# A first stage that also builds other layers' conditioning: 21 background chunks moved forward, and the ring of tiles split in two

## The chip, the cores and the metric

The kernel runs on one core of one Trainium2 chip. The metric is the device time of one execution in microseconds (us), the median of several runs. Lower is better. TensorE is called PE here, VectorE DVE, ScalarE ACT, GpSimd POOL and SyncE SP, as in the profile.

## The reference: what is computed

A backbone block with two layers works on 256 noisy latent tokens and 256 context tokens of width 2048. Every layer's modulation comes from a conditioning vector:

```python
def ada_mods(cvec, w, b):
    m = jax.nn.silu(cvec) @ w + b
    return jnp.split(m, N_MOD, axis=-1)
```

The first two parts (shift and scale of layer 0's mixer) are needed before anything else: the normalised input is `h * (1 + scale) + shift`, and the first layer's projections multiply that by large weight matrices. The other parts of the same kind (gate, and the shift, scale and gate of the two feed-forward blocks and of layer 1) are needed only later in the program, one after another. Layer 0 then runs eight HGRN2 heads (query, forget gates, values, a chunked scan) beside token-mixing heads, an output projection and a feed-forward block; layer 1 a pooling mixer and a feed-forward block.

## The kernel before

All large products are made in three passes of a reduced float format: a weight tile `raw` arrives from HBM by DMA, ACT casts it to a high part `hi`, DVE subtracts to get the low part `lo` (`load_w`, lines 169 to 187), and PE multiplies high by high, high by low and low by high (`mm`, line 221). A raw tile's buffer can be filled again when its `hi` and `lo` are made. All these DMAs are issued by SP, whose queue takes them strictly in order: one that must wait for its buffer holds back all behind it.

**The first stage** (`startup`, lines 438 to 609) goes through the 16 k-tiles of the input in nine slices: two slices of one k-tile, then seven of two. It overlaps two things. For slice i it computes with PE the first projections (`values`, two groups v0 and v1 with PSUM tiles `mmi`; `forgets`, three groups f0, f1, f2 with tiles `mmf`). Meanwhile it prepares slice i+1: `cond` multiplies the conditioning vector by the weights of shift and scale (tiles `sraw`, 512 KB each, PSUM tile `ps_as`), `transposed` turns the input, and `modulate` brings both together into the k-tiles `xt` that the next v0 reads. A slice of two k-tiles needs eight `sraw`: four in group A (run 0 of `cond`), four in group B (run 1). Within a group PE takes the tile that was loaded last first. The order on PE is written out by hand: v0, A, v1, B with the transposes, f0, the small products of `modulate`, f1, f2; for i = 1 alone it is v0, A, B, v1, so A and B stand back to back. `in_order` ties each step to the one before. All other engines are filled by a scheduler by priority; `high_priority(offset=-LATER)` marks work that is to come last.

The `sraw` tiles and the background's tiles share one ring of seven buffers, tag `a4`; two more buffers, tag `s4`, serve `sraw` in the first stage alone. So `sraw` go round nine buffers.

**The background** (`ada_task`, lines 296 to 339) makes the parts of the modulation that are needed later: 20 tasks of 16 chunks each, 320 in all. A chunk is one DMA of 512 KB (`araw`, line 307) and one DVE instruction that adds `araw` times a scalar to an accumulator `acc` (line 311). After the 16th chunk `last` splits `acc` into two tiles `apart` and sends them through PE. Chunks are taken from a list by `pump`, which `load_w` calls: each load adds `rate` to a credit, and each whole credit takes a chunk, at low priority. `plan(left, loads)` sets the rate so that after so many loads only `left` chunks remain. The heads (`mixer_even`) begin with

```python
        self.plan(LEFT_H, LOADS_H)
```

with LEFT_H = 240 and LOADS_H = 22: 80 chunks over 22 loads. After them `plan(LEFT_M, 38)` takes 50 more over 38 loads. In the first stage the rate is zero: no chunk is taken there.

Of the kernel before, what the change touches and what calls it, by code (L numbers as in the profile page):

```python
# [12 lines left out]
F32 = mybir.dt.float32  # L13
F32R = mybir.dt.float32r
# [5 lines left out]
P = 128  # L20
# [10 lines left out]
LATER = 50  # L31
# [2 lines left out]
STEPS = "f0 f1 f2 q0 s0 i s1 q1 f3 s2 f4 s3 q2 f5 s4 f6 s5 q3 f7 s6"  # L34
LOADS_H = 8 + 4 + 2 * (NH - N_START)
BATCH = 2
NA4 = 7
NS4 = 2
NG4 = 7
NT2 = 9  # L40
N_PRE = 3
FIRST_S = 100
HELD = 1
N_WARM = 1
N_WARM_S = 15
LEFT_H = 240
LEFT_M = 190
# [103 lines left out]
class Builder:  # L151
# [141 lines left out]
    def ada_task(self, task, dst, row):  # L293

        nc = self.nc
        st = {}

        def first():
            st["acc"] = self.ap.tile([P, 1024], F32, tag="a4", bufs=NA4, name="acc")
            nc.gpsimd.memset(st["acc"], 0.0)  # L300
            nc.sync.dma_start(st["acc"][0:1, :], self.I["bada"][task:task + 1, :])

        def chunk(c):
            if c == 0:
                first()
            raw = self.ap.tile([P, 1024], F32, tag="a4", bufs=NA4, name="araw")
            nc.sync.dma_start(raw, self.I["wada"][task * 16 + c])
            acc = st["acc"]

            with self.tc.issue_after(self.norm) if self.norm is not None else nullcontext():  # L310
                nc.vector.scalar_tensor_tensor(acc, raw, self.csil[:, c, 0:1], acc, ALU.mult, ALU.add)  # L311
            if c == KT - 1:
                last()

        def last():
            hi, lo = (self.ap.tile([P, 1024], F32R, tag="a4", bufs=NA4, name="apart") for _ in range(2))
            nc.scalar.copy(hi, st["acc"])
            nc.vector.tensor_sub(lo, st["acc"], hi.bitcast(F32))
            if row:
                g = self.gate_tile()  # L320
                dst.append(g)
                for j in range(2):
                    ps = self.pa.tile([P, 512], F32, tag="ax", name="ps_ada")
                    for i, z in enumerate((hi, lo)):
                        self.mm(ps, self.ones, z[:, 512 * j:512 * j + 512], i == 0, i == 1)
                    nc.scalar.copy(g[:, 512 * j:512 * j + 512], ps)
            else:
                ps = self.pa.tile([P, 512], F32, tag="ax", name="ps_ada")
                rows = self.cp.tile([4, T], F32, tag="crow", bufs=1, name="crow")
                for j in range(4):  # L330
                    for i, z in enumerate((hi, lo)):
                        self.mm(ps[0:4, 0:T], self.hot[:, j], z[:, T * j:T * j + T], j + i == 0, j + i == 4)
                nc.scalar.copy(rows, ps[0:4, 0:T])
                for h in range(2):
                    nc.tensor.transpose(ps[:, T + 4 * h:T + 4 * h + 4], rows[:, h * P:h * P + P], self.ident[0:4, 0:4])
                nc.scalar.copy(dst.rearrange("p (j h) -> p h j", h=2), ps[:, T:T + 8].rearrange("p (h j) -> p h j", h=2))

        for c in range(KT):
            self.bg.append((task // 2, lambda c=c: chunk(c)))
# [100 lines left out]
    def startup(self):  # L440
# [8 lines left out]
        for b in range(4):  # L449
            src = (I["x"] if b < 2 else I["ctx"])[(b % 2) * P:(b % 2) * P + P, :]  # L450
            if b < 2:
                t = self.xp.tile([P, D], F32, tag="x8", name="xraw")
# [43 lines left out]
        def cond(i, run):  # L496
# [8 lines left out]
            for c in range(run * nk, run * nk + nk):  # L505
                src = I["wada_h"][2 * k0 + c] if nk == 1 else I["wada_s"][2 * k0 - 4 + c]
                for h in range(2):
                    self.n_sraw += 1
                    if self.n_sraw % (NA4 + NS4) < NS4:
                        t = self.sp.tile([P, 1024], F32, tag="s4", bufs=NS4, name="sraw")  # L510
                    else:
                        t = self.ap.tile([P, 1024], F32, tag="a4", bufs=NA4, name="sraw")
                    nc.sync.dma_start(t, src[:, 1024 * h:1024 * h + 1024])
                    todo += [(n * c + j, t, j * w % 1024) for j in range(n) if j * w // 1024 == h]
            first = None
# [94 lines left out]
        def in_order(*steps):  # L610
            for fn in steps:
                with self.tc.issue_after(st["last"]) if "last" in st else nullcontext():
                    fn()
                st["last"] = self.first_mm
# [3 lines left out]
        for i, (k0, nk) in enumerate(slices):  # L618
# [10 lines left out]
            steps += [lambda: forgets(i, 0, wf)] + more * [lambda: modulate_first(i + 1)]  # L629
            steps += [lambda h=h: forgets(i, h, wf) for h in range(1, N_START)]  # L630
            in_order(*steps)
            if i in (1, 4):
                with self.tc.issue_after(st["act"]), self.tc.issue_after(st["dve"]):
                    scale_rows(1) if i == 1 else self.lower_bounds()
# [459 lines left out]
    def build(self):  # L1094
        nc, tc = self.nc, self.tc
        pool = tc.tile_pool
        with pool(name="cp", bufs=1) as self.cp, pool(name="wp", bufs=1) as self.wp, \
# [7 lines left out]
            c = {n: col(n) for n in ("sh2_0", "sc2_0", "sh1_1", "sc1_1", "sh2_1", "sc2_1")}  # L1105
            self.NG4, self.NT2 = NG4, NT2
            with pool(name="tp0", bufs=1) as self.tp, pool(name="vp", bufs=1) as self.vp:
# [8 lines left out]
                self.ada(8, c["sc2_1"])  # L1116
                gate2 = self.ada(9, None)
                with pool(name="sp", bufs=1) as self.sp:
                    fbacc = self.startup()
                with pool(name="gp", bufs=1) as self.gp:  # L1120
                    self.mixer_even(fbacc)
                    stat = self.out_proj()
# [31 lines left out]
```

## Time and profile before

| | before |
|---|---|
| median of 3 runs | 2271.59 us (2270.16 to 2273.35) |
| the profiled execution | 2277.5 us |
| its span in the trace | 2275.4 us |
| PE busy, share of the span | 2244.2 us, 99% |
| DVE busy | 1686.8 us, 74% |
| ACT busy | 1101.7 us, 48% |
| HBM read | 578.55 MB, 255 GB/s over the span |

The profiled execution took 5.9 us more than the median of the runs; 2.1 us of its time lie outside its span. In the trace the first stage runs from the start to about 174 us, the heads from there to about 478 us, the token mixing to about 545, the output projection to 685, the first feed-forward block to 1409, the pooling mixer to 1552, the last feed-forward block to the end. A busy PE is not a PE at its peak, but a stretch in which PE is busy throughout can't be shortened by anything that another engine does sooner.

### The profile page before, as it was taken

What the parts mean: (1) busy time and instruction counts of PE and PEld (TensorE: products, weight loads), DVE (VectorE), ACT (ScalarE), POOL (GpSimd) and SP (SyncE); (2) the same over time, 40 slices, a digit from 0 to 9 for tenths busy, and PEclk for the clock granted to TensorE, in tenths of its full rate; (3) what the DMA queues carried; (4) which work ended last, traced back from release to release, by engine and by line L of the source; (5) the groups of instructions that cost most, each with busy time, mean ns of one, the idle gap of its engine ahead of it and who ended that gap; (6) DMA issues with size and microseconds to landing.
All of it is one profiled execution on the core that took longest, in us unless ns stands there. A gap on an engine that the chain in (4) does not pass through costs nothing.

```text
span 2275.4 us, 31649 instructions
## 1 busy us (share of the span) xinstructions
PE 2244.2 (99%) x12532; PEld 1866.1 (82%) x12532; DVE 1686.8 (74%) x2055; ACT 1101.7 (48%) x1484; POOL 37.0 (2%) x47
## 2 busy tenths in 40 slices
PE   9999999999999999999999999999999999999998
PEld 5677788778888878888887888888888888888887
DVE  4669999988868877887888875769964655556655
ACT  4326466554446545544544554445444443443443
POOL 0000000001000000000000000000000000000000
PEclk9999999999999999999999999999999999999999
DMA  9786766777877888888888885646865555555553
GB/s 376 279 300 224 273 254 245 263 278 289 323 278 264 317 307 304 302 319 304 314 317 308 296 307 197 222 171 250 313 228 194 185 187 196 182 192 187 185 190 125
DMA packets 110636, 582.71 MB, mean 256 GB/s; under 512 B 12292, under 2 KB 12420, under 8 KB 66584
## 3 DMA queue, kind: packets, MB, share of 16 engines
q1 hardware_dynamic: 110488, 580.70, 70.4%
q8 instruction: 98, 1.61, 0.3%
q14 instruction: 50, 0.41, 0.0%
HBM read 578.55 MB, written 2.10 MB: 255 GB/s over the span
## 4 chain that ended last, share of the span: by engine, by line
PE 82%; DVE 8%; DMA 5%; issue 2%; ACT 2%; POOL 0%; SPq 0%; DVEq 0%; POOLq 0%; ACTq 0%
PE mma L221 36%; PE mmb L221 34%; PE mmf L221 3%; PE mmn L221 2%; DMA araw<-in_wada 2%; DVE lo L185 2%; DVE acc L311 2%; PE mmi L221 2%; PE ps_as L221 1%; ACT hi L184 1%; DVE kk L758 1%; DVE qg L758 1%; DMA sraw<-in_wada_h 1%; PE ps_ada L221 0%; PE ps_o L221 0%
## 5 line engine op out<-in xcount | busy, mean ns | idle before, releaser
L184 ACT CAST hi<-raw 128x1024 fp32r<-128x1024 f32 (+1 forms) x701 | 733.0, 1047 | 942.1 <-PE mma L221 461.0
L185 DVE TENSOR_TENSOR lo<-raw,hi 128x1024 fp32r<-128x1024 f32 (+1 forms) x701 | 849.8, 1215 | 408.5 <-ACT hi L184 407.0
L221 PE MATMUL mma<-hi,xt 128*128 128x512 f32 x2800 | 873.3, 391 | 0.9 <-DVE q L280 0.9
L221 PE MATMUL mmb<-xt,hi 128*128 128x512 f32 x2304 | 812.8, 397 | 1.1 <-DVE xt L389 0.8
L221 PE MATMUL mmb<-xt,lo 128*128 128x256 f32 x2304 | 648.0, 281 | 0.8 <-DVE lo L185 0.8
L221 PEld LDWEIGHTS mma<-hi,xt 128*128 128x128 f32 x2800 | 525.0, 188 | 111.8 <-DVE q L280 1.3
L221 PE MATMUL mma<-lo,xt 128*128 128x512 f32 x1400 | 547.1, 391 | 2.1 <-DVE lo L185 2.1
L221 PEld LDWEIGHTS mmb<-xt,hi 128*128 128x128 f32 x2304 | 432.8, 188 | 103.8 <-DVE xt L389 1.0
L311 DVE SCALAR_TENSOR_TENSOR acc<-araw,csil,acc 128x1024 f32<-128x1024 f32 x320 | 409.9, 1281 | 62.1 <-DMA araw<-in_wada 59.7
L221 PEld LDWEIGHTS mmb<-xt,lo 128*128 128x128 f32 x2304 | 436.3, 189 | 3.1 <-DVE lo L185 1.1
L221 PEld LDWEIGHTS mma<-lo,xt 128*128 128x128 f32 x1400 | 263.2, 188 | 58.5 <-DVE lo L185 3.2
L221 PE MATMUL mmf<-xt,hi 128*128 128x512 f32 x512 | 165.3, 395 | 0.1
L221 PEld LDWEIGHTS mmf<-xt,hi 128*128 128x128 f32 x512 | 96.0, 188 | 21.0 <-PE mmf L221 0.5
L221 PE MATMUL mmf<-xt,lo 128*128 128x512 f32 x256 | 100.1, 391 | 0.0
L221 PE MATMUL mmn<-hi,xt 128*128 128x256 f32 x416 | 76.0, 283 | 0.0
L221 PEld LDWEIGHTS mmn<-hi,xt 128*128 128x128 f32 x416 | 65.3, 192 | 0.4
L221 PE MATMUL mmn<-lo,xt 128*128 128x256 f32 x208 | 58.9, 283 | 0.0
L221 PEld LDWEIGHTS mmf<-xt,lo 128*128 128x128 f32 x256 | 48.2, 188 | 9.5
L740 ACT COPY both<-kk 128x256 f32<-128x256 f32 x64 | 26.3, 411 | 54.2 <-DVE kk L758 43.3
L389 DVE TENSOR_TENSOR xt<-hup,xt 128x512 fp32r<-128x512 f32 x64 | 43.9, 687 | 7.9 <-ACT xt L388 7.9
L603 DVE TENSOR_TENSOR fbacc<-mmf,fbacc 128x1024 f32<-128x1024 f32 x24 | 29.3, 1221 | 21.9 <-PE mmf L221 21.8
L221 PE MATMUL mmi<-hi,xt 128*128 128x512 f32 x128 | 44.2, 404 | 1.2 <-DVE xt L568 0.6
(187 smaller groups left out, 1347.1 us busy)
## 6 DMA issues: line engine op xcount, KB each, us to landing
araw<-in_wada SPq DMA_DIRECT2D x320, 512.0 KB
raw<-in_w_up SPq DMA_DIRECT2D x128, 1024.0 KB
raw<-in_w_down SPq DMA_DIRECT2D x128, 1024.0 KB
sraw<-in_wada_s SPq DMA_DIRECT2D x56, 512.0 KB
raw<-in_w_out SPq DMA_DIRECT2D x16, 1024.0 KB
raw<-in_w_pool SPq DMA_DIRECT2D x16, 1024.0 KB
raw<-in_w_fb SPq DMA_DIRECT2D x10, 1024.0 KB
raw<-in_w_q SPq DMA_DIRECT2D x8, 1024.0 KB
```

The lines of the kernel that those rows point to most:

```text
L184: nc.scalar.copy(hi, raw[:, o:o + w])
L185: nc.vector.tensor_sub(lo, raw[:, o:o + w], hi.bitcast(F32))
L221: self.first_mm = self.nc.tensor.matmul(out, lhsT, rhs, start=start, stop=stop, **kw).ins
L311: nc.vector.scalar_tensor_tensor(acc, raw, self.csil[:, c, 0:1], acc, ALU.mult, ALU.add)
L389: return self.nc.vector.tensor_sub(x[:, :, lo], src, x[:, :, hi].bitcast(F32))
L603: nc.vector.tensor_add(fbacc[h], ps, fbacc[h])
L740: nc.scalar.copy(o.rearrange("p (s j i) -> p j s i", j=2, i=hh), bass.AP(src.tensor, src.offset, [list(src.ap[0]), [st + hh, 2], [seg, ns] ...
L758: nc.vector.tensor_mul(x, x, m.broadcast_to([P, ns, hh]))
```

## The change

The ring `a4` goes from seven buffers to three. A new ring `b4` has four, so both together take as much memory as before. The ring `s4` of the first stage goes from two buffers to three. In the first stage the `sraw` tiles use `b4` and `s4`, seven buffers together, and background chunks use `a4`, where one buffer is held by the accumulator. After the first stage a chunk with an odd number uses `a4`, one with an even number `b4`; the two `apart` tiles use `b4`.

At the end of the iterations i = 2 to 8 of the first stage three chunks each are taken from the list at low priority, 21 in all. The plan of the heads still leaves 240, so its 22 loads now take 59 chunks and not 80.

```diff
-NA4 = 7
-NS4 = 2
+NA4 = 3
+NB4 = 4
+NS4 = 3
...
+N_EARLY = 3
...
         def chunk(c):
             if c == 0:
                 first()
-            raw = self.ap.tile([P, 1024], F32, tag="a4", bufs=NA4, name="araw")
+
+            ring = ("a4", NA4) if self.first_stage or c % 2 else ("b4", NB4)
+            raw = self.ap.tile([P, 1024], F32, tag=ring[0], bufs=ring[1], name="araw")
             nc.sync.dma_start(raw, self.I["wada"][task * 16 + c])
...
         def last():
-            hi, lo = (self.ap.tile([P, 1024], F32R, tag="a4", bufs=NA4, name="apart") for _ in range(2))
+            hi, lo = (self.ap.tile([P, 1024], F32R, tag="b4", bufs=NB4, name="apart") for _ in range(2))
...
                     self.n_sraw += 1
-                    if self.n_sraw % (NA4 + NS4) < NS4:
+                    if self.n_sraw % (NB4 + NS4) < NS4:
                         t = self.sp.tile([P, 1024], F32, tag="s4", bufs=NS4, name="sraw")
                     else:
-                        t = self.ap.tile([P, 1024], F32, tag="a4", bufs=NA4, name="sraw")
+                        t = self.ap.tile([P, 1024], F32, tag="b4", bufs=NB4, name="sraw")
...
             in_order(*steps)
+            if i >= 2:
+                with self.tc.high_priority(offset=-LATER):
+                    for _ in range(N_EARLY):
+                        self.bg.popleft()[1]()
...
+                    self.first_stage = True
                     fbacc = self.startup()
+                    self.first_stage = False
```

Three places show how the instructions move. Names carry the program's numbers; line numbers after the change are larger by 2 to 8.

SP's queue before, at the loads of one slice of the first stage (the slice whose `ps_as` ran at 112.01 us in the trace of before). The waits in brackets are on semaphores: PE_49 is set by PE, DVE_49 by DVE, Activation_49 by ACT, DMAHW by earlier transfers of the same number:

```order
L174 DMA raw_949<-in_w_is 128x1024 [waits DMAHW1_49,DVE_49]
L174 DMA raw_955<-in_w_fbs 128x1536 [waits DMAHW2_49,DVE_49]
L513 DMA sraw_980<-in_wada_s 128x1024 [waits DMAHW3_49,PE_49]
L513 DMA sraw_982<-in_wada_s 128x1024 [waits DMAHW4_49,PE_49]
L513 DMA sraw_984<-in_wada_s 128x1024 [waits DMAHW5_49,PE_49]
L513 DMA sraw_986<-in_wada_s 128x1024 [waits DMAHW6_49,PE_49]
L513 DMA sraw_1010<-in_wada_s 128x1024 [waits DMAHW7_49]
L513 DMA sraw_1012<-in_wada_s 128x1024 [waits DMAHW0_49,PE_49]
L513 DMA sraw_1014<-in_wada_s 128x1024 [waits DMAHW1_49]
L513 DMA sraw_1016<-in_wada_s 128x1024 [waits DMAHW2_49]
L174 DMA raw_1099<-in_w_is 128x1024 [waits DMAHW3_49,DVE_49]
```

The eight tiles of the slice, sraw_980 to sraw_986 for group A and sraw_1010 to sraw_1016 for group B, stand together, and each one's wait on PE is for tiles of the slice before.

SP's queue after, at the same slice, from the third tile of group A on (group A is sraw_1010 to sraw_1016 here, group B sraw_1040 to sraw_1046):

```order
L517 DMA sraw_1014<-in_wada_s 128x1024
L517 DMA sraw_1016<-in_wada_s 128x1024 [waits DMAHW5_49,PE_49]
L517 DMA sraw_1040<-in_wada_s 128x1024 [waits DMAHW7_49,DMAHW6_49]
L517 DMA sraw_1042<-in_wada_s 128x1024
L517 DMA sraw_1044<-in_wada_s 128x1024 [waits DMAHW0_49]
L311 DMA araw_960<-in_wada 128x1024 [waits DMAHW1_49,DVE_49]
L311 DMA araw_963<-in_wada 128x1024 [waits DMAHW2_49,DVE_49]
L517 DMA sraw_1046<-in_wada_s 128x1024 [waits DMAHW3_49,PE_49]
L311 DMA araw_966<-in_wada 128x1024 [waits DMAHW4_49,DMAHW1_49,DVE_49]
L176 DMA raw_1138<-in_w_is 128x1024 [waits DMAHW5_49,Activation_49]
L176 DMA raw_1144<-in_w_fbs 128x1536 [waits DMAHW6_49,Activation_49]
```

The eighth tile of the slice, sraw_1046, now stands behind two chunks and takes the buffer of sraw_1010, so its wait on PE is for the fourth pair of matmuls of group A of its own slice. The third chunk and the weights of the next slice stand behind it.

ACT before, at the last but one step of `modulate` (xt6 is k-tiles 12 and 13; the inputs of the casts L184 are the weights w_fbs and w_is of the next slices):

```order
L540 COPY sp_1200<-ps_as_1129 128x512
L557 ACTIVATE mtmp_1211<-ps_t_1176,mcol_1207 128x256 x2
L567 CAST xt6_98<-mtmp_1211 128x512
L567 CAST xt6_98<-mtmp_1212 128x512
L184 CAST hi_1257<-raw_1255 128x1024
L184 CAST hi_1261<-raw_1255 128x512
```

ACT after, at the same place:

```order
L544 COPY sp_1239<-ps_as_1168 128x512
L186 CAST hi_1299<-raw_1297 128x1024
L561 ACTIVATE mtmp_1250<-ps_t_1215,mcol_1246 128x256
L186 CAST hi_1305<-raw_1303 128x1024
L561 ACTIVATE mtmp_1250<-ps_t_1215,mcol_1246 128x256
L186 CAST hi_1309<-raw_1303 128x512
L571 CAST xt6_98<-mtmp_1250 128x512
L571 CAST xt6_98<-mtmp_1251 128x512
```

The two casts that make xt6 have moved behind both casts of the weights raw_1303; the buffers that those write are read by PE until the last matmul of f2.

DVE after, at the same step:

```order
L563 TENSOR_SCALAR mtmp_1251<-ps_t_1216,mcol_1246 128x256
L187 TENSOR_TENSOR lo_1306<-raw_1303,hi_1305 128x1024
L187 TENSOR_TENSOR lo_1310<-raw_1303,hi_1309 128x512
L563 TENSOR_SCALAR mtmp_1251<-ps_t_1216,mcol_1246 128x256
L572 TENSOR_TENSOR xt6_98<-mtmp_1250,xt6_98 128x2x256
L607 TENSOR_TENSOR fbacc_214<-mmf_1274,fbacc_214 128x1024
L572 TENSOR_TENSOR xt6_98<-mtmp_1251,xt6_98 128x2x256
```

The low parts of raw_1303 stand ahead of the two instructions that finish xt6, and the addition of f2's result between those two. The same order returns at the step after it (xt7).

## Rows read from the trace of the kernel before

**Rows 1.** Windows: length, busy us per engine, PE clock (1.00 is full), DMA share, GB/s.

```profile
20.00:48.00 28.00, 27.20 (x181) 17.34 (x179) 12.66 (x25) 13.14 (x20) 0.00 (x0) 1.00 1.03 403
48.00:168.00 120.00, 119.61 (x655) 82.98 (x655) 76.82 (x105) 38.12 (x56) 0.95 (x1) 1.00 0.81 297
168.00:478.00 310.00, 301.41 (x2385) 244.51 (x2385) 292.90 (x553) 181.73 (x352) 7.89 (x7) 1.00 0.70 252
sum 2275.40, PE 2244.21 PEld 1866.08 DVE 1686.76 ACT 1101.65 POOL 36.98; mean PE 249.36 PEld 207.34 DVE 187.42 ACT 122.41 POOL 4.11
```

**Rows 2.** Waits of PE over the span: us in total, times, longest us.

```profile
PE ps_sc L221 <- ACT both L740: 5.9, 9, 1.5
PE ps_mx L221 <- DVE vg L843: 3.0, 2, 2.1
```

**Rows 3.** Timeline of one slice: start us, us, engine, line, operation.

```profile
92.42 1.92 PE L221 MATMUL ps_as<-sraw,cst 128*32 128x512 f32 x16
...
97.26 1.92 PE L221 MATMUL ps_as<-sraw,cst 128*32 128x512 f32 x16
...
107.82 1.28 DVE L568 TENSOR_TENSOR xt<-mtmp,xt 128x512 fp32r<-128x512 f32 x2
...
109.20 0.39 PE L221 MATMUL mmi<-hi,xt 128*128 128x512 f32 x1
...
112.01 1.50 PE L221 MATMUL ps_as<-sraw,cst 128*32 128x512 f32 x12
```

**Rows 4.** Timeline where groups A and B stand back to back.

```profile
37.82 1.92 PE L221 MATMUL ps_as<-sraw,cst 128*32 128x512 f32 x16
...
39.91 1.50 PE L221 MATMUL ps_as<-sraw,cst 128*32 128x512 f32 x12 [0.17 <-DMA sraw<-in_wada_s]
```

**Rows 5.** Timeline with SP's issues (SPq), and the PE group before the first.

```profile
53.28 1.92 PE L221 MATMUL ps_as<-sraw,cst 128*32 128x512 f32 x16
...
54.38 5.68 SPq L513 DMA_DIRECT2D sraw<-in_wada_s  x6
...
91.39 0.33 SPq L174 DMA_DIRECT2D raw<-in_w_fbs  x1
...
99.24 1.29 SPq L513 DMA_DIRECT2D sraw<-in_wada_s  x3
```

**Rows 6.** Chain of waits: start us, us from issue to landing.

```profile
0.74 4.86 DMA xraw<-in_x
...
835.09 5.75 DMA araw<-in_wada
...
1413.53 5.85 DMA raw<-in_w_pool
```

**Rows 7.** Windows behind the issue at 91.39, columns as in Rows 1.

```profile
91.90:92.90 1.00, 1.00 (x11) 0.35 (x13) 0.97 (x2) 0.00 (x0) 0.00 (x0) 1.00 0.49 123
92.90:93.90 1.00, 1.00 (x16) 0.23 (x8) 0.85 (x1) 0.00 (x0) 0.00 (x0) 1.00 0.89 326
```

**Rows 8.** Windows from the longest wait of PE on.

```profile
527.80:530.20 2.40, 0.31 (x2) 0.18 (x2) 0.87 (x4) 1.04 (x1) 1.78 (x1) 1.00 0.59 150
530.20:533.60 3.40, 3.40 (x14) 3.19 (x15) 2.70 (x8) 0.00 (x0) 0.00 (x0) 0.50 1.01 419
```

**Rows 9.** Timeline at the last step of `modulate`.

```profile
167.77 0.62 ACT L567 CAST xt<-mtmp 128x512 fp32r<-128x512 f32 x1
167.91 1.83 DVE L185 TENSOR_TENSOR lo<-raw,hi 128x1024 fp32r<-128x1024 f32 x2
...
168.29 0.62 ACT L184 CAST hi<-raw 128x512 fp32r<-128x512 f32 x1
...
169.65 0.69 DVE L568 TENSOR_TENSOR xt<-mtmp,xt 128x512 fp32r<-128x512 f32 x1
...
170.25 1.22 DVE L603 TENSOR_TENSOR fbacc<-mmf,fbacc 128x1024 f32<-128x1024 f32 x1
```

**Rows 10.** Groups of instructions: count, busy us, mean ns, idle before.

```profile
L311 DVE SCALAR_TENSOR_TENSOR acc<-araw,csil,acc 128x1024 f32<-128x1024 f32 x320 | 409.9, 1281 | 62.1 <-DMA araw<-in_wada 59.7 <-DMA acc<-in_bada 0.2
```

## The prediction, made before the result was known

> **What bounds the kernel now.** I read the windows by stage first. PE is busy for 2244.21 of 2275.40 us, so only 31 us can be won by waits that go away [rows 1]. In the steady part of the first stage PE is busy for 119.61 of 120 us, while DVE is busy for 76.82 and the DMA engines for 0.81 of the time; in the heads PE is busy for 301.41 of 310, DVE for 292.90 [rows 1]. The reader is to see two different stages: in the first, spare time lies on DVE (43 us in 120) and no wait of PE is left; in the heads DVE is nearly full, and PE waits 8.6 us. The waits of PE come next: the longest sum is that of the score products for ACT's copies, 5.9 us in nine waits, and the longest single one 2.1 us, in the token mixing [rows 2]. Last comes the timeline of one slice, since the change sets new waits there: A starts at 92.42, B at 97.26, v0 of the next slice at 109.20, and the next A at 112.01 [rows 3]. So a slice takes 19.6 us of dense PE work, B starts 4.84 us after A, and whatever comes late to A, B or v0 adds to the total one to one.
>
> **What is taken from the heads.** 21 chunks leave the plan of the heads, 1.28 us of DVE each [rows 10], 27 us at most. This is no gain by itself: DVE has to become late for PE to wait, and PE's waits in the heads are 8.6 us in all [rows 1], so 8.6 is the upper end. The order of the instructions tells less: between the same two weight splits of the heads (the 24th and the 78th `lo` of the program) DVE carries 87 chunks before and 82 after, because low-priority chunks run ahead of their plan when their buffers allow. Five chunks are 6.4 us of DVE. If DVE's saving came back to PE by the share in which PE waits there (8.6 of 310), it would be 0.2 us; if all of it came back, 6.4. The score products wait for ACT's copies, which wait for DVE's, in nine places only. I take a gain of 1 us, with -8.6 and +3 as ends (the latter half of the waits of the score products again, if these products, which stand closer together in the new order, find their copies later).
>
> **What the chunks cost in the first stage.** 21 chunks are 27 us of DVE and 21 x 512 KB of DMA, three per slice. DVE has 43 us free in 120. A slice moves eight `sraw` of 512 KB, 512 KB of w_is and 768 KB of w_fbs: 10.5 units of 512 KB, and 13.5 with three chunks. At the 403 GB/s of the window from 20 to 48 us [rows 1], where the queue is full, a unit takes 1.30 us, so a slice takes 13.7 us before and 17.6 after, of its 19.6. It fits, with 2 us to spare. PE does nothing for them. As work the chunks cost nothing; the cover is DVE's idle time and those 2 us.
>
> **Term 1, the shorter ring.** Before, nine buffers serve the eight tiles of a slice, and every tile waits for tiles of the slice before. After, seven serve eight: the eighth tile takes a buffer of group A of its own slice. It is the tile that PE takes first in B. So its load can start only when PE has used that buffer in A, and has to land before B, which starts 4.84 us after A begins. Which of the four it waits for is read from the semaphores of the program: in the seven slices of two k-tiles the fourth used, first, second, third, fourth, second, third. The delay from the start of A to the issue is in two rows: 1.10 us for the first used (53.28 to 54.38) and 1.98 us for the fourth (97.26 to 99.24) [rows 3, 5]; 1.4 and 1.7 lie between.
>
> How long 512 KB take from the issue on an empty queue no row shows alone. Three come near: 1 MB took 4.86 and 5.85, and 512 KB in a stretch of other traffic 5.75 [rows 6]. Without the 1.30 us of the second half the first two give 3.6 and 4.55; I take 4.1, their middle. The low end is from the bytes: after the issue at 91.39 on an idle queue 123 KB had moved by 92.90 and 449 by 93.90, so 524 can't be there before 94.1, 2.7 us after [rows 5, 7]. The high end is 5.75.
>
> A page of the Trainium skill has another price. "DMA: Bandwidth & Descriptors", section "Anatomy of one DMA — SWDGE (gpsimd) path", gives about 2.0 us plus the bytes over 436 GB/s, so 3.2 us for 512 KB as an estimate (for DMAs issued by GpSimd; these are SP's). By it this term would be 0.5 for the six steady slices and 3.1 for the first, 3.6 us and not 8.9.
>
> With 4.1, B is late by (issue + 4.1 - 4.84): 0.36, 0.66, 0.96 and 1.26 us for first to fourth. The six steady slices give 0.36 + 0.66 + 0.96 + 1.26 + 0.66 + 0.96 = 4.9 us (0 at 2.7; 14.8 at 5.75). The first of the seven is worse, since there A and B stand back to back, at 37.82 and 39.91 [rows 4]. Its eighth tile is issued at 37.82 + 1.98 = 39.80 and lands at 43.9: B is 4.0 us late (2.6 at 2.7; 5.65 at 5.75). What is late next behind the waiting DMA in SP's queue is the next slice's w_fbs and `sraw`; they are needed 13 us later and more, so nothing follows from it.
>
> **Term 2, the clock behind the first wait.** A wait of 2.1 us was followed by 3.4 us at half clock, 0.50 granted (1.2 of 2.4 GHz), and behind waits up to 1.5 us in the heads the clock was not lowered (1.00) [rows 1, 2, 8]. So the 4 us at 40 may cost 3.4 / 2 = 1.7 us more. I take 1.7; ends 0 and 3.4.
>
> **Term 3, the order of the last two steps of `modulate`.** In a steady slice xt is ready at 107.82 + 1.28 = 109.10 and v0 starts at 109.20 [rows 3]: 0.1 us of slack. For xt6 and xt7 the new order puts both casts of xt behind the second cast of w_fbs, whose buffer is free only when f2 has ended; call that E. From E: cast 0.62, casts of xt 0.62 each, so v0 starts at E + 1.24 and not at E; on DVE `lo` (about 0.65 for its 512 columns) ends at 1.3, the last half of mtmp at 1.8, the first xt at 2.5, the addition of f2 at 3.7, the second xt at 4.4 [rows 9]. v0 has 12 matmuls in 2.8 us (109.20 to 112.01, [rows 3]): two run at 1.24, the third waits for 2.5, the second k-tile's last four wait for 4.4 and end at 5.5 or so, against 2.8 without a delay. With the time of the semaphores between, 2.9 us are lost at xt6. At xt7 the order of before is half turned already (`lo`, then xt, [rows 9]), and loses 0.3 to 0.6 there, so 2.3 are new. Together 5.2 us (low end 4.6). These waits come in pieces of 1.3 us and less, so I charge no clock for them.
>
> **Sum.** 4.0 + 4.9 + 1.7 + 5.2 - 1 = +14.8 us, against the profiled execution's 2277.5 (span 2275.4): 2292.3. That execution is 5.9 us over the median of the three runs; what lies between is not in these terms, so I add the sum to the median, 2271.6 + 14.8 = 2286.4.
>
> **Rivals.** (a) The transfers land sooner. At 2.7 us the steady waits vanish and 2.6 us stay in the first slice, with no lower clock; with 4.6 of term 3 and 3 us won in the heads the time is 2271.6 + 2.6 + 4.6 - 3 = 2275.8. For it: nothing but the bytes had moved after 2.7; against it: all three landings of [rows 6]. The Trainium skill's price (above) would make it 2281, between this and the sum.
>
> (b) Faster than before. The heads are paced by DVE: at 292.90 of 310 it is the fullest engine beside PE, and its queue is in order, so chunks between two head steps delay those. Then all 8.6 us of PE's waits go. It decides once the first stage loses less than that, by 4 us at least: loads at 2.7 us with xt6 and xt7 finished on time, because the scheduled order costs little where f2 is late anyway. Time 2271.6 - 8.6 + 1 = 2264. Against it: five chunks fewer, not 21, and the slack of 0.1 us at v0.
>
> (c) The chunks' DMAs throttle SP's queue. One waits for the addition before it (DVE), and holds back w_fbs and the next group A. At the step of xt6 the third chunk of a slice waits for an addition that DVE makes only behind v1: the first chunk lands behind the eighth tile, 1.4 + 4.1 + 1.3 = 6.8 us after A, its addition takes 1.28, so the third is issued 8.1 us after A and not 2. That takes 6.1 us of a queue with 2 to spare: 4.1 us in up to six slices, 25 us, and with terms 1 and 2 of the first slice about 2271.6 + 25 + 5.7 = 2302. For it: DVE's order after the change; against it: where term 3 delays PE, the queue gains the same time, and only that step has its addition so late.
>
> (d) The change does nothing at that place: excluded, SP's order shows the chunks between the `sraw`. A split ring could hold up the later stages; there 3 + 4 buffers stand for 7, and by the order the additions return to the old places after about 150 chunks, so I take no cost.
>
> **Numbers.** My sum 0.58; (a) 0.20; (b) 0.10; (c) 0.12. The range from 2270 to 2297 holds all of (a) and the sum with its transfers up to 5 us; below it lies most of (b), above it (c). A change of 0.2%, 4.5 us, is about what a measurement of this kernel can tell from none. (a) is half within that bound and half above it; so faster 0.11, same 0.14, slower 0.75.
>
> **What would show it.** In the new trace PE's waits in the first stage should name `ps_as` waiting for the DMA of `sraw`: about 4 us at 40, and 0.4 to 1.3 us in each slice after; `mmi` waiting for xt (ACT, then DVE) at the two last slices, 2 to 3 us each; a granted clock under 1 in the 3 us after 44. The heads' PE wait falls from 8.6 by 1 or so. The end of the first stage moves from about 174 to about 190. It is wrong if `ps_as` shows no wait for DMA behind the first slice (a), if the heads shorten by over 5 us (b), or if PE waits for hi of w_fbs or for group A (c).

## The result, and the profile after

| | before | after |
|---|---|---|
| median of 4 runs | 2272.41 us (2270.16 to 2273.35) | 2298.69 us (2294.29 to 2302.62) |
| ratio, with its 95% interval | 1 | 1.0112 [1.0099, 1.0125] |
| the profiled execution | 2277.5 us | 2294.29 us |
| its span | 2275.4 us | 2292.5 us |

The changed kernel is slower by 26 us; +14.8 was forecast, so the sign was right and the size too small. The two profiled executions are no fair pair: that of before lay 5 us above its kernel's median, that of after is the lowest of its four. A second profile of before (e5 below) took 2270.39 us with a span of 2268.4, 2 us under the median; shifts of instructions are counted from that one.

The page's first part for the kernel after shows PE busy as long as before, to 1 us, in a span that is 17 us longer:

```profile
PE 2245.3 (98%) x12532; PEld 1865.0 (81%) x12532; DVE 1685.1 (74%) x2055; ACT 1102.9 (48%) x1484; POOL 36.4 (2%) x47
```

So the loss lies in waits. The windows of the same stretches as in [rows 1] say in which stage (the later stretches hold other work now, since all is 20 us later):

```profile
20.00:48.00 28.00, 22.86 (x150) 12.88 (x149) 8.94 (x18) 12.18 (x19) 0.00 (x0) 0.94 0.92 352
48.00:168.00 120.00, 111.37 (x599) 76.58 (x598) 83.68 (x108) 34.59 (x50) 0.00 (x0) 0.99 0.84 301
168.00:478.00 310.00, 298.38 (x2269) 241.33 (x2262) 283.67 (x537) 177.46 (x343) 8.29 (x7) 1.00 0.71 252
```

In the steady first stage PE had been idle for 0.4 of 120 us and is now idle for 8.6; in the 28 us before, 5.1 after 0.8. DVE has 83.68 us of work there after 76.82: 12 additions of chunks lie in this window after 4, and DVE is still free for 36 us. The waits of PE over the whole span name the releaser (before first, then three rows of after):

```profile
PE ps_as L221 <- DMA sraw<-in_wada_s: 0.2, 1, 0.2
...
PE ps_as L223 <- DMA sraw<-in_wada_s: 11.9, 7, 4.3
...
PE mmi L223 <- ACT xt L571: 2.6, 2, 1.3
...
PE mmi L223 <- DVE xt L572: 1.6, 3, 0.7
```

Seven waits for `sraw`, one in each slice of two k-tiles, of together 11.9 us where there was one of 0.2, and the waits for the late xt. How such a wait comes about is read from the timeline (SPq is SP's queue; the number in brackets is the idle time ahead). First where A and B stand back to back, then two steady slices:

```profile
36.95 1.92 PE L223 MATMUL ps_as<-sraw,cst 128*32 128x512 f32 x16
...
38.93 0.33 SPq L517 DMA_DIRECT2D sraw<-in_wada_s  x1
...
43.15 3.51 PE L223 MATMUL ps_as<-sraw,cst 128*32 128x512 f32 x16 [4.28 <-DMA sraw<-in_wada_s]
...
77.22 0.33 SPq L176 DMA_DIRECT2D raw<-in_w_fbs  x1
...
78.25 1.92 PE L223 MATMUL ps_as<-sraw,cst 128*32 128x512 f32 x16
...
79.37 0.33 SPq L517 DMA_DIRECT2D sraw<-in_wada_s  x1
...
85.16 1.92 PE L223 MATMUL ps_as<-sraw,cst 128*32 128x512 f32 x16 [2.00 <-DMA sraw<-in_wada_s]
...
121.02 1.92 PE L223 MATMUL ps_as<-sraw,cst 128*32 128x512 f32 x16
...
123.00 0.33 SPq L517 DMA_DIRECT2D sraw<-in_wada_s  x1
...
127.52 1.93 PE L223 MATMUL ps_as<-sraw,cst 128*32 128x512 f32 x16 [1.59 <-DMA sraw<-in_wada_s]
```

Each time SP issues an `sraw` 1 to 2 us after A has begun: the eighth tile, which waited for a buffer of A. B starts 4.2 to 5.8 us behind that issue. All seven slices, from the same timeline (us; late is B minus A minus the 4.84 of [rows 3], for the first minus 2.09 of [rows 4]):

| A starts | eighth tile issued | B starts | issue to B | B late by |
|---|---|---|---|---|
| 36.95 | 38.93 | 43.15 | 4.22 | 4.1 |
| 58.09 | 59.18 | 63.51 | 4.33 | 0.58 |
| 78.25 | 79.37 | 85.16 | 5.79 | 2.07 |
| 99.92 | 101.87 | 106.27 | 4.40 | 1.51 |
| 121.02 | 123.00 | 127.52 | 4.52 | 1.66 |
| 142.25 | 143.38 | 147.75 | 4.37 | 0.66 |
| 166.65 | 168.60 | 172.94 | 4.34 | 1.45 |

The windows show the granted clock behind two of the waits, at 40 us and at xt6:

```profile
43.20:47.00 3.80, 3.80 (x19) 0.95 (x20) 0.00 (x0) 0.29 (x1) 0.00 (x0) 0.55 1.01 397
47.00:50.00 3.00, 3.00 (x18) 2.60 (x17) 0.84 (x1) 1.14 (x2) 0.00 (x0) 1.00 0.77 254
162.60:166.00 3.40, 3.40 (x9) 2.61 (x10) 1.66 (x2) 0.00 (x0) 0.00 (x0) 0.53 0.75 305
184.00:190.00 6.00, 3.96 (x15) 2.37 (x14) 5.23 (x8) 2.89 (x5) 0.00 (x0) 1.00 0.58 211
```

Near half (the lower level, 1.2 of 2.4 GHz) for 3.8 us behind the wait of 4.28 us, and again for 3.4 us behind the waits of xt6; at xt7 (the last row), with waits as long (1.28 and 0.68 us), it was full. The timeline of xt6 itself:

```profile
160.48 0.62 ACT L571 CAST xt<-mtmp 128x512 fp32r<-128x512 f32 x1
161.15 0.50 PE L223 MATMUL mmi<-hi,xt 128*128 128x512 f32 x1 [1.31 <-ACT xt L571]
161.84 0.68 DVE L572 TENSOR_TENSOR xt<-mtmp,xt 128x512 fp32r<-128x512 f32 x1
162.58 1.05 PE L223 MATMUL mmi<-hi,xt 128*128 128x512 f32 x2 [0.70 <-DVE xt L572]
```

PE waits first for ACT's cast, then for DVE's subtraction: the two waits that the orders of ACT and DVE had shown, 1.31 and 0.70 us. In the second trace of the changed kernel (e1 below) they are 1.32 and 0.69 us, and the clock behind them was full:

```profile
163.50:167.00 3.50, 3.43 (x18) 1.84 (x22) 2.21 (x3) 0.00 (x0) 0.00 (x0) 1.00 0.68 276
```

### The profile page after: what moved, and what is told of

Same layout as the page of the kernel before. It is cut to its first block, busy times and chain, and to the rows that moved or that the text cites. A ratio compares the mean times of both kernels' runs of the same rounds, so it can differ in the third digit from the quotient of the medians.

```text
span 2292.5 us, 31645 instructions
## 1 busy us (share of the span) xinstructions
PE 2245.3 (98%) x12532; PEld 1865.0 (81%) x12532; DVE 1685.1 (74%) x2055; ACT 1102.9 (48%) x1484; POOL 36.4 (2%) x47
## 4 chain that ended last, share of the span: by engine, by line
PE 83%; DVE 8%; DMA 5%; issue 2%; ACT 2%; POOL 0%; SPq 0%; DVEq 0%; POOLq 0%; ACTq 0%
PE mma L223 39%; PE mmb L223 33%; PE mmn L223 3%; PE mmf L223 2%; DVE acc L315 2%; DVE lo L187 2%; DMA araw<-in_wada 2%; DMA sraw<-in_wada_s 1%; PE ps_as L223 1%; PE mmi L223 1%; DVE qg L766 1%; DVE kk L766 1%; ACT hi L186 1%; PE ps_ada L223 1%; DMA raw<-in_w_pool 1%
## 5 line engine op out<-in xcount | busy, mean ns | idle before, releaser
L223 PE MATMUL ps_as<-sraw,cst 128*32 128x512 f32 (+1 forms) x288 | 32.8, 575 | 12.0 <-DMA sraw<-in_wada_s 11.9
```

The lines of the kernel that those rows point to most:

```text
L223: self.first_mm = self.nc.tensor.matmul(out, lhsT, rhs, start=start, stop=stop, **kw).ins
```

## Experiments

The theory behind the prediction was that the ring of seven causes most of the loss, the turned order of `modulate`'s last two steps the rest, and that the chunks themselves and the heads count for little. Its rivals were that the chunks' DMAs hold up SP's queue, that the heads give time back, and, after the result, that the split of the ring costs in the later stages. Shifts in the text are the later start of one instruction against the trace of e5: of the first product of w_q, with which the first stage ends, of the heads' last forget products, of the start of the first feed-forward block, and of the end. Single traces of one kernel differ by up to 7 us behind the first stage (the two of before), so small shifts there mean nothing.

**e1 and e5, both kernels again**, unaltered.

> The changed kernel once more, unaltered, for a second profile and the granted clock of each run. Theory A (the three terms, of which the clock's is drawn anew in each execution): median 2296 to 2301 us; in the trace the same seven waits of PE for sraw (11 to 13 us together) and the same late xt6 and xt7 to 0.3 us, but other windows with a clock under 1 behind the long waits; runs with a lower mean clock are longer by about (difference of clock) x 2300 us. Theory B (something in the later stages differs from run to run): the profile's first stage is the same, clock and all, and the difference lies behind 480 us.

> The kernel before once more, unaltered, for a second profile, since its first profiled execution is 6 us longer than the median of its runs (2271.3). Theory A (the first profile of before was a long execution): span about 2269.5, mean clock 0.999, and by matching instructions the first profile loses its 6 us in places that have nothing to do with the change: the start, a wait and half clock at 528 to 534, the rest spread. Then the changed kernel's trace lies 23 us behind this one, most of it before 205 us. Theory B: the second profile is as long as the first.

e1: 2296.32 us beside 2271.27, ratio 1.011 [1.0097, 1.0123]. e5: 2273.05 beside 2272.71, 1.0004 [0.9993, 1.0014]. The result stands at +25. Against e5 the first profile of before is 2.8 us late at the heads' end and 7.1 at the end. In two traces each, the loss lies here (us late at the four places): after 19.9, 19.7, 22.8, 24.1; e1 19.6, 21.5, 27.2, 26.9. So 20 us are lost in the first stage, where the two traces of before agree to 0.03 us, and none are won in the heads that can be told from none. Behind the heads these traces show 4.4 and 5.4 us, but the first profile of before is 4.3 us late there too. What tells of a loss there is the medians: 25 to 26 us in all (22 to 28 by the interval of e1) leave some 5 to 6 beside the first stage's 20.

**e2, the rings without the chunks.**

```diff
-N_EARLY = 3
+N_EARLY = 0
```

> The split rings alone, no chunk in the first stage (N_EARLY 0, 80 chunks in the heads as before). Theory A: the ring's waits and the clock behind the first, 12 to 15 us over before (2284 to 2288), seven waits of PE for sraw of together 10 to 12 us, xt6 and xt7 in time. Theory B (the chunks' DMAs and additions cost it, the ring little): under 4 us over before.

2294.16 us, ratio 1.0097 [1.0083, 1.0112]: the rings alone cost nearly all of it, 20.4 us of it by the first product of w_q. Its waits of PE, and the timeline of one of its slices:

```profile
PE ps_as L223 <- DMA sraw<-in_wada_s: 17.5, 7, 5.6
...
122.45 1.92 PE L223 MATMUL ps_as<-sraw,cst 128*32 128x512 f32 x16
...
123.54 0.33 SPq L517 DMA_DIRECT2D sraw<-in_wada_s  x1
...
123.97 0.80 SPq L176 DMA_DIRECT2D raw<-in_w_fbs  x1
...
132.95 1.94 PE L223 MATMUL ps_as<-sraw,cst 128*32 128x512 f32 x8 [5.59 <-DMA sraw<-in_wada_s]
```

The chain of that stretch names the eighth tile (start of the issue, us to the landing):

```profile
124.86 8.05 DMA sraw<-in_wada_s
```

The waits are longer than with chunks, 17.5 against 11.9 us. Here the scheduler has put a tile of the next slice and w_fbs (issued at 123.54 and 123.97) ahead of the eighth tile, and it lands after 8.05 us, not 4.3. The parts of the loss are others: B is late by 13.4 us in the six steady slices and not 7.9, and behind the wait at 132.95 the clock takes 1.7 us more; the order of `modulate` takes nothing, and 6.6 in the changed kernel. That both first stages end nearly alike (20.4 and 19.9 us late) is chance, as far as these traces tell. It is shown that the ring by itself costs as much in this stage as the whole change; what the chunks add or save depends on where the scheduler puts the other loads beside them.

**e6 and e4, a ring of eight.** Eight buffers for `sraw`, in the same memory; chunks have two, one of which the accumulator holds. e6 is without chunks in the first stage, e4 with three.

```diff
-NA4 = 3
-NB4 = 4
+NA4 = 2
+NB4 = 5
```

> a4 2, b4 5, s4 3 and no chunk in the first stage: eight buffers for sraw, the split rings in the later stages, 80 chunks in the heads. Theory A (the loss of the split is the tile that waits for its own slice): within 4 us of before, no wait of PE for sraw over 0.3 us behind 45 us. Theory B (the split costs in the later stages, where odd chunks have one ring and even ones another): the first stage as before, 8 us or more lost behind 200 us.

> The changed kernel with a4 2, b4 5, s4 3: eight buffers for sraw, one for a chunk beside the accumulator; 21 early chunks as in the change. Theory A: no wait of PE for sraw behind 45 us, and by the new order only half of xt is late, at xt4 to xt7, 0.5 to 1.5 us each: 2 us under to 5 us over before. Theory B (the chunks throttle SP's queue, now with one buffer even more): PE waits for sraw or w_fbs, 10 us or more over before.

e6: the first stage ends 1.3 us sooner than in e5, so with eight buffers for eight tiles nothing is lost there: the missing eighth buffer is the whole of the ring's cost in that stage. Yet its time is 2293.03 us, 1.0095 [1.0078, 1.0112]: it is 3.6 us late at the heads' end, 15.5 at the feed-forward block and 18.7 at the end. e4: 2296.25, 1.011 [1.0087, 1.0134], with runs from 2288 to 2307, and 9.0 us late in the first stage. PE's waits there (from 30 to 200 us) are for `sraw` and, by the turned order again, for xt and for the addition of f2's result; SP's queue (36 to 205 us) is held by the chunks:

```profile
PE ps_as L223 <- DMA sraw<-in_wada_s: 4.2, 6, 1.0
PE mmi L223 <- DVE xt L572: 2.7, 5, 0.6
PE mmi L223 <- DVE fbacc L607: 1.1, 1, 1.1
...
SPq L311 <- DMA araw<-in_wada: 34.2, 10, 6.8
```

The same row of the changed kernel is:

```profile
SPq L311 <- DMA araw<-in_wada: 8.4, 3, 3.9
```

So three chunks a slice that wait for each other for one free buffer hold SP's queue, and `sraw` come late. That is 4.2 us of e4's loss at the most (1.0 of it lies in the slice ahead of the first chunk); the turned order takes up to 3.8. With two free buffers, as in the change, no wait of PE for group A or for weights shows.

**e3 and e7, the order mended.** xt is placed ahead of the next weights' casts, in e3 in the changed kernel, in e7 with eight buffers and two chunks a slice.

```diff
+            if i >= 2:
+                self.hold = [[], [st["act"], st["dve"]], [st["act"], st["dve"]]]
```

> The changed kernel with the casts of w_fbs tied behind the last xt of each slice (hold in load_w), so that xt6 and xt7 come first again. Theory A: 5 to 8 us less than the changed kernel (4.0 and 2.5 in its trace, the lower clock behind xt6 included), the seven waits for sraw unchanged. Theory B (the late xt only takes the place of loads that come late too): the waits move to sraw or w_fbs, under 2 us less.

> Eight buffers for sraw, two chunks in each slice and not three, casts of w_fbs tied behind xt: the version that theory A would build. Theory A: SP is held less by the single buffer for chunks than in e4, xt is in time; 3 us under to 6 us over before, 10 us and more under the changed kernel. Theory B (a chunk between the loads of a slice always holds SP's queue): as e4, 15 us or more over before, PE waiting for sraw in the last slices.

e3: 2288.64 us, 1.0077 [1.0065, 1.0089], 8 to 10 us better than the changed kernel. The waits for xt at xt6 and xt7 are gone (its profiled execution, the longest of its five, shows 3.8 us of the gain in the first stage); but the hold, which starts at i = 2, makes a new one in the slice after:

```profile
56.84 0.50 PE L223 MATMUL mmi<-hi,xt 128*128 128x512 f32 x1 [1.77 <-ACT xt L571]
```

The next A is 9.2 us late there, against 5.3 without it, and the whole first stage 16.1 against 19.9. Part of that is the clock: in this trace it was at half for 6.8 us from 41.5 us on, not for 3.4, and again for 3.4 behind the new wait. e7 below has the same wait at full clock. e7 loses 1.6 us in the first stage (1.4 by this wait), so two chunks a slice are nearly free with eight buffers; its time is 2297.16, 1.0111 [1.0095, 1.0127], again through what follows: 13.9 at the heads' end, 17.7 and 23.2 behind.

**e8, PE kept busy through the wait at 40**, by 16 products of zeros (32 matmuls in the trace) that nothing uses, between A and B.

```diff
-            steps = v0 + c0 + c1 + v1 if i == 1 else v0 + c0 + v1 + c1
+            steps = v0 + c0 + [lambda: fill(16)] + c1 + v1 if i == 1 else v0 + c0 + v1 + c1
```

> The changed kernel with 16 products of zeros, not used, between A and B of the slice where these stand back to back, about the length of the wait there; its new order also brings xt6 and xt7 back in front, so it is to be compared with e3 (2288.6 us). Theory A (the lower clock behind the first wait is set off by PE's idleness): clock 1.00 behind 43 us, the seven waits as before but the first under 1 us, 2 to 4 us less than e3. Theory B (the clock falls for another reason): half clock there as in e3, no gain.

```profile
42.15 7.17 PE L223 MATMUL ps_warm<-idle,ident 128*128 128x256 f32 x32
44.00:46.00 2.00, 2.00 (x11) 1.77 (x10) 0.00 (x0) 0.00 (x0) 0.00 (x0) 1.00 0.83 207
```

The clock stayed full here, where it fell in all five traces with PE idle (after, e1, e2, e3, e9); so it was the idle time that had lowered it. From the start of B to the next A it is 13.33 us (49.25 to 62.58), in e5 13.31 and in after 14.94: 1.6 us for the clock. The whole time, 2301.9 us, 1.0131 [1.0112, 1.015], doesn't tell it: the products took 7.2 us where 4 were to be filled, and A came 3 us later in the new order.

**e12, the heads alone**: before, with 21 chunks moved out of the heads to later stages.

```diff
-LEFT_H = 240
+LEFT_H = 261
```

> The kernel before with LEFT_H 261: 59 chunks in the heads and not 80, as in the change, the 21 put behind the heads, the first stage untouched. It measures by itself what the heads give back. My term: 0 to 2 us less between the heads' start and 425 us, and 0 to 3 us more behind. Rival (b) (the heads are paced by DVE): 5 us or more less in the heads.

2278.98 us, 1.0028 [1.0016, 1.0039]: 6.6 us over before. The first product of w_q starts 0.65 us sooner than in e5 and the last forget products 0.36 sooner. But the heads are no lighter than before. Between these two places DVE makes as many additions as ever, since chunks of a later plan move up; e5, e12 and the changed kernel, in this order:

```profile
L311 DVE SCALAR_TENSOR_TENSOR acc<-araw,csil,acc 128x1024 f32<-128x1024 f32 x74 | 94.4, 1276 | 1.0 <-DMA araw<-in_wada 0.9
L311 DVE SCALAR_TENSOR_TENSOR acc<-araw,csil,acc 128x1024 f32<-128x1024 f32 x73 | 93.4, 1280 | 3.8 <-DMA araw<-in_wada 3.4
L315 DVE SCALAR_TENSOR_TENSOR acc<-araw,csil,acc 128x1024 f32<-128x1024 f32 x77 | 98.3, 1276 | 4.4 <-DMA araw<-in_wada 4.2
```

The plan moves 21 chunks, the execution of e12 one and that of the change none: it makes 10 additions more ahead of the heads and 3 more in them. So e12 does not measure what lighter heads give back, and where its 6.6 us go is not shown.

**e13, the split alone**: the changed rings, but `sraw` goes round all ten buffers and no chunk is early.

```diff
-                    if self.n_sraw % (NB4 + NS4) < NS4:
+                    at = self.n_sraw % (NA4 + NB4 + NS4)
+                    if at < NS4:
                         t = self.sp.tile([P, 1024], F32, tag="s4", bufs=NS4, name="sraw")
+                    elif at < NS4 + NB4:
+                        t = self.ap.tile([P, 1024], F32, tag="b4", bufs=NB4, name="sraw")
                     else:
-                        t = self.ap.tile([P, 1024], F32, tag="b4", bufs=NB4, name="sraw")
+                        t = self.ap.tile([P, 1024], F32, tag="a4", bufs=NA4, name="sraw")
```

> The rings of the change (a4 3, b4 4, s4 3, odd and even chunks apart behind the first stage), but in the first stage sraw goes round all ten buffers and no chunk is taken there. It measures by itself what the split costs behind the first stage. Theory A with a split that costs 3 to 5 us later: 2 to 6 us over before, first stage as before to 1 us, the loss between 200 and 1450 us. Theory A alone (all of the change's loss is in the first stage): within 1.5 us of before. Theory D (the split is what costs; the first stage's waits would only be made up for later): 12 us or more over before.

2275.04 us, 1.0008 [0.9998, 1.0017]: no loss in the first stage (0.6 us sooner than e5), and in all 2.3 us that a measurement can't tell from none (3.9 at the most, by the interval).

**e9, e10, e11, the split made less even.** In e9 the changed kernel with every third chunk in the ring of three (two of them free) instead of every second; e10 and e11 are e6 and e7 with every sixth in the ring of two (one free), e11 with the hold from i = 5 on.

```diff
-            ring = ("a4", NA4) if self.first_stage or c % 2 else ("b4", NB4)
+            ring = ("a4", NA4) if self.first_stage or c % 6 == 0 else ("b4", NB4)
```

> The changed kernel with one thing altered behind the first stage: of the chunks every third takes a4, whose two free buffers are a third of the six, and not every second. Theory C (after e6: a ring whose buffers don't match its share of the chunks holds SP's queue; in the change the two free buffers of a4 take half of the chunks): the part of the loss that lies behind 200 us, about 4 us in its trace against the second one of before, goes, the first stage stays: 2 to 5 us under the changed kernel. Theory A alone (all is lost in the first stage): no difference beyond 1.5 us.

> As e6 (eight buffers for sraw, no chunk in the first stage) but behind the first stage every sixth chunk takes a4, whose one free buffer is a sixth, and not every second. Theory C: the 18 us that e6 lost behind 200 us go, but for 0 to 4; total within 4 us of before. The other theory (the split as such, or the place of the accumulator, costs in the later stages): 10 us or more over before, as e6.

> The version that the runs point to: eight buffers for sraw, two chunks in each slice, casts of w_fbs behind xt from the sixth slice on, behind the first stage every sixth chunk in a4. By theories A and C together: first stage 0 to 3 us over before, heads 0 to 3 us under, the rest as before: 2 us under to 4 us over before. If the heads were paced by DVE (rival b): 4 us or more under before.

e9: 2303.01 us, 1.0136 [1.0122, 1.015], so for the rings of the change the idea fell: it is 30.3 us late at the end, not less. Of these, 23.4 lie in the first stage, which the edit leaves as it is: there one eighth tile came into use 6.67 us after its issue, not 4.33, and the clock fell behind that wait. Behind the first stage e9 loses 6.9 us, the changed kernel 4.2 and 7.3 in its two traces. e10: 2284.17, 1.0053 [1.0041, 1.0066]; e11: 2284.06, 1.0058 [1.0044, 1.0071]: 9 and 13 us better than e6 and e7 (1.7 of the 13 lie in the first stage, where the hold differs). So with rings of two and five it had cost that much to give half of the chunks to the one free buffer. In e11 the first stage with its 14 chunks takes as long as in e5 (0.1 us sooner at w_q) and the heads 1.0 us less. Both lose 13.6 and 14.7 us behind the heads in their traces all the same. DVE's wait for chunks, in the group that answers to [rows 10], does not tell the time here; e6 first, then the faster e10:

```profile
L315 DVE SCALAR_TENSOR_TENSOR acc<-araw,csil,acc 128x1024 f32<-128x1024 f32 x320 | 409.4, 1279 | 75.7 <-DMA araw<-in_wada 73.6 <-issue 0.3
```

```profile
L315 DVE SCALAR_TENSOR_TENSOR acc<-araw,csil,acc 128x1024 f32<-128x1024 f32 x320 | 409.8, 1281 | 109.2 <-DMA araw<-in_wada 107.1 <-issue 0.6
```

**e14, one shared ring**: before, with ten buffers instead of nine, two chunks a slice and the mended order from i = 5.

```diff
-NS4 = 2
+NS4 = 3
...
+            if i >= 5:
+                self.hold = [[], [st["act"], st["dve"]], [st["act"], st["dve"]]]
```

> The kernel before with its one shared ring (a4 7) and s4 3, ten buffers for sraw, two chunks in each slice from the third on at low priority out of the same ring, casts of w_fbs behind xt from the sixth slice on, 66 chunks in the heads. If chunks in the first stage are free there as in e11 and the later stages keep the ring of before: within 3 us of before, or under it by up to 3. If moving chunks forward costs in later stages whatever the ring (as moving them back did in e12): 5 us or more over before. If chunks in the shared ring take sraw's buffers: PE waits for sraw in the first stage, 5 us or more there.

```profile
PE ps_as L221 <- DMA sraw<-in_wada_s: 1.8, 3, 1.0
```

2272.45 us beside 2272.72, 1.0001 [0.9991, 1.001]: 14 chunks can be moved forward without loss, and nothing comes of it: 1.5 us later at w_q (its waits for `sraw` between 36 and 205 us are above), 1.3 sooner at the heads' end, and the same time. Its heads are 2.8 us shorter than in e5, as much as those of the first profile of before are longer. No kernel tried here beats the kernel before.

## Why the prediction was too low

**The ring, first slice** (4.0 forecast): 4.1, with the eighth tile issued at the delay read from [rows 3] and landed in 4.22 us.

**The ring, six steady slices** (4.9): 7.9, the sum of the table's last six rows, and 8.5 in e1. The step that failed is the landing of "4.1, their middle": it was 4.3 to 4.5 us in five slices and 5.79 in one (6.41 in e1), where w_fbs had been issued 2.1 us ahead of the tile. Over 4.1 these give 3.2 us more (0.23 + 1.69 + 0.30 + 0.42 + 0.27 + 0.24). The delays taken as 1.4 and 1.7 us were 1.1 and 1.95, which cancel to 0.1 in the sum (and the 1.26 there should read 1.24). The prediction's "empty queue" was none in that slice; which load stands ahead of the eighth tile could be read from the order, but not its price. In the traces of e1, e2, e3, e8 and e9 too, a tile with nothing issued in the 4.5 us ahead of it was in use 4.1 to 4.5 us after its issue; with w_fbs 1.9 to 2.2 us ahead it was 4.6 to 6.9, with w_fbs 3.0 us ahead 4.1 to 6.7. The second slice, with the same loads ahead, had 4.33 in after and 6.67 in e9 (59.32 to 65.99):

```profile
56.28 0.35 SPq L176 DMA_DIRECT2D raw<-in_w_fbs  x1
...
59.32 1.85 SPq L517 DMA_DIRECT2D sraw<-in_wada_s  x4
...
65.99 0.64 PE L223 MATMUL ps_as<-sraw,cst 128*32 128x512 f32 x4 [2.88 <-DMA sraw<-in_wada_s]
```

What decides between these stays open. The Trainium skill's price, in "DMA: Bandwidth & Descriptors", section "Anatomy of one DMA — SWDGE (gpsimd) path", which is stated for GpSimd's DMAs, gives 3.2 us as an estimate; no tile that PE waited for here came under 4, so the traces do not agree for SP's.

**The clock at 40** (1.7): 3.8 us at 0.55, so 3.8 x 0.45 = 1.7, and e8 has that time back.

**The order of `modulate`** (5.2): 6.6, of which 4.1 at xt6 and 2.5 at xt7; in e1 5.5, of which 3.0 at xt6. In the trace of after the failing step is "I charge no clock for them": at xt6 two waits of 1.31 and 0.70 us, with one matmul between them, were followed by 3.4 us at 0.53, that is 1.6 us; at xt7 1.28 and 0.68 were not. In e1 the same two waits were not followed by it either, and there xt6 lost 3.0 for the 2.9 forecast. So this term was sized about rightly, but for a clock that fell in one of the two traces.

These four make 20.3 us; the first stage measured 20.3 (19.92 + 0.39, since group A at 37 us was 0.39 sooner than in e5). 15.8 were forecast. e1 comes to nearly the same, 19.7, by other parts: more for the ring, less for the order.

**The heads** (-1): -0.25 in the trace of after, +1.9 in that of e1, against +2.8 in the first trace of before. Nothing that can be told from zero. The step "21 chunks leave the plan of the heads" did not come about: between the first product of w_q and the last forget product DVE makes 77 additions after 74 (the rows at e12). The prediction's order of instructions had warned of it, with five chunks fewer and not 21. What heads with clearly fewer chunks would win is not shown.

**Behind the heads** ("I take no cost"): 4.4 us in after, 5.4 in e1, about as much as the two traces of before differ there (4.3); by the medians 5 to 6 us are lost beside the first stage. So this step failed too, and its cause stays open. e13 shows that the split itself, with the chunks in their old places, gives 2.3 us that can't be told from none. A split with one free buffer (e10, e6) costs 13.6 and 15.1 us there in its traces, so a ring that is too small for its chunks does lose time behind the heads. That the changed kernel's rings do so is not shown, and in e9 another share of the chunks for each ring won nothing.

**The rivals.** (a), sooner landings: excluded by the table. (b), faster heads: they were not faster, but its condition was not met either, since DVE had no fewer additions there. In e4 it had 66, for 74 before, and the heads took 1.9 us longer in its trace; with another ring that argues against (b) and does not exclude it. (c), SP's queue: its third chunk was issued 8.2 us after A as worked out (142.25 to 150.44, below), yet PE waited for no group A; its time, 2302, was the nearest, by luck. With one free buffer e4 shows `sraw` late behind a held queue, 4.2 us at the most.

```profile
142.25 1.92 PE L223 MATMUL ps_as<-sraw,cst 128*32 128x512 f32 x16
...
150.44 0.33 SPq L311 DMA_DIRECT2D araw<-in_wada  x1
```

So the mechanisms of the first stage were right and the landing's size was wrong, the gain in the heads had no ground, and a cost behind them had been put at nothing. In the trace of after 3.0 us for the landing, 1.4 for the order with its clock, 0.7 for the heads and 4.4 behind them make 9.5 of the 9.7 us between 14.8 and the 24.5 (24.1 at the end and the 0.4 by which A was early) that it shows against e5. That this comes out so closely is partly luck: after's trace is 4.4 us under its kernel's median and e5 2 us under its own, and by the medians 10 to 11.5 us were missing.

## What to carry to other kernels

A ring with fewer buffers than one step uses turns a load of that step into a wait, whatever the mean load of the queue: the price is issue plus landing minus the time until the tile is used, in every step, and one buffer more takes it to nothing. Work that is moved into another engine's idle time is worth only what its old place paid for it. Count in the new trace whether it has left that place at all: where a scheduler lets work run ahead of its plan, other work moves up. Take the landing from a load that stands behind the same neighbours in the queue, with a range of some us even then, and take a second profile of both kernels when terms of a few us are weighed.

## What the runs showed of the hardware

Where PE waited for them, 512 KB issued by SP were in use 4.1 to 4.5 us after the issue with nothing issued in the 4.5 us ahead, 4.6 to 6.9 with 768 KB issued 1.9 to 2.2 us ahead, 4.1 to 6.7 with 768 KB 3.0 us ahead (after, e1, e2, e3, e8, e9), and landed after 8.1 with 512 and 768 KB issued 1.3 and 0.9 us ahead (e2). The clock does not fall the same way each time: behind the waits of 1.31 and 0.70 us at xt6 it fell to 0.53 in after, behind 1.32 and 0.69 at the same place in e1 it did not, nor behind 1.28 and 0.68 at xt7. In before, the half clock of [rows 8] behind a wait of 2.1 us is missing in e5, where the same product waited 1.9 us:

```profile
478.00:545.00 67.00, 64.25 (x308) 52.45 (x307) 58.45 (x102) 29.52 (x33) 7.61 (x4) 1.00 0.81 305
PE ps_mx L221 <- DVE vg L843: 2.8, 2, 1.9
```

And the kernel before, whose runs agree within 0.4%, gave two profiled executions 7.1 us (0.3%) apart, none of it in the first stage.
